# Opening of a two-layer hybrid decoder: lambda's vectors inside the packed parameters, first modulation tiles ahead of x, first norm by full products of ones

## The chip, the cores and the metric

One core of a Trainium2 chip runs the whole program. The metric is device time in microseconds (us) for one execution. Engines are named as in the profile: PE (TensorE matmul), PEld (its weight loads), DVE (VectorE), ACT (ScalarE), POOL (GpSimd), SP (SyncE, which here only issues DMAs).

## What is computed

Two layers of a trunk over a 256 x 1024 activation `x`, batch 1. Only the first steps of the first layer matter for the change; the rest is a sentence each.

```python
mod = silu(c) @ w_ada[l] + b_ada[l]                      # 1024 -> 6 x 1024: shift, scale, gate, twice
h = rmsnorm(x, norm1_g[l]) * (1 + sc1) + sh1
proj = h @ w_in[l]                                       # 1024 -> 2560: SSM input, two attentions' q, k, v
lam = exp(sum(lq1 * lk1)) - exp(sum(lq2 * lk2)) + lam_init   # a number per layer, vectors of 64
# S5 state space mixer, differential attention (uses lam), MoBA attention, w_out, gate, residual
# second norm with its own shift and scale, squared-ReLU MLP 1024 -> 4096 -> 1024, gate, residual
# after both layers: rmsnorm(x, final_g)
```

The decay factors of the state space mixer come from small parameter vectors (`a_re`, `a_im`, `log_dt`) by exponentials and sines.

## The kernel before

The activation is kept transposed: `xall` has 128 partitions, 8 feature tiles (`KT` = 8) and 256 time steps. A weight comes as a unit of 128 x 1024 fp32 (512 KB), loaded by SP into one of three `raw` buffers (L109). Each unit is split into a rounded high part (ACT, L123) and the remainder (DVE, L124), the activation likewise (`h_tile`, L432), and three products replace one fp32 product (`mm3`, L129).

All parameter vectors stand in one packed tile `par` (L72, columns given by `_COLS`). The lambda vectors do not: L1020 loads them with a DMA on ACT's queue that reads one row of 2 KB for each of the 128 partitions, and `ssm_params` multiplies and sums them on DVE (L498, L500), then feeds one exponential (`small_exp`, L502) that also yields the decay factors.

The opening runs over k = 0 to 7 (L1044). In round k, `ada_first(k)` (L318) loads two tiles of the modulation weights (buffers `ada`, three of them, `adaacc`, one, and `qT`, three, in turn), multiplies them on PE by the replicated silu(c) (`crep`) in four column strips, and ACT copies the result to `adarow`. `sums` brings it to columns of `mod`. `h_first(k-1)` builds the normed tile of the round before, and `proj_first(k-2)` adds its three groups of projections. On PE the order is: modulation of round k, projection of round k-2, sums of round k; so the first projection stands behind the modulation of the third round.

The first norm needs the mean square of x over features, which lie on partitions. `ssq_add` (L371) squares each of eight tiles on ACT and multiplies by ones, packed into four column strips of PE. `rms_bcast` (L380) copies the four partial sums, brings them to two columns by small matmuls with `sel` (L387), takes the root there (`rsqrt_cols`, ACT and four tiny DVE operations), and spreads the result by two transposes (L392) over all rows of a PSUM tile `pb`. Later norms use `x_norm` (L408): full products with a 128-column matrix of ones that put the sum in every row at once, one reciprocal root over 128 x 256 on ACT (L426) and a Newton step of three DVE operations over 128 x 256 (L427 to L429).

SP issues loads in the order of the program: `par`, four pieces of `x` (L78, 256 KB each), then for each round two modulation tiles (L330) and one weight unit (L109), each as its buffer comes free. A scheduler orders the other engines' instructions by when it believes that their inputs are ready, so small parameter work (`rope_tables`, `ssm_params`, L456 and L483, which stand behind the loop in the program) is spread between the opening's instructions on DVE. An engine's queue runs strictly in the order given.

Of the kernel before, what the change touches and what calls it, by code (L numbers as in the profile page):

```python
# [10 lines left out]
F32 = mybir.dt.float32  # L11
# [3 lines left out]
OP = mybir.AluOpType  # L15
# [26 lines left out]
for _name, _w in (("c", 8), ("a_re", 16), ("a_im", 16), ("ldt", 16), ("n1", 16), ("n2", 16), ("b_ada", 96),  # L42
                  ("d", 4), ("glu_b", 4), ("ssm_g", 4), ("subln", 2), ("moba", 2), ("fin", 8)):
    _COLS[_name] = (_n, _n + _w)
    _n += _w
# [8 lines left out]
@with_exitstack  # L54
def hybrid_trunk(ctx, tc, xT_d, pos_d, par_d, lqk_d, sb_d, sbt_d, scw_d, glu_d, wm_d, wa_d, out_d):
    nc = tc.nc
# [19 lines left out]
    xall = const.tile([128, KT, S], F32)  # L76
    for k in range(0, KT, 2):
        nc.sync.dma_start(xall[:, k:k + 2, :], xT_d[:, k:k + 2, :])  # L78
    xT = [xall[:, k, :] for k in range(KT)]
# [235 lines left out]

    last_row = [None]

    def ada_first(k):  # L318


        row = wk_tile()[:, :256]
        for h in range(2):
            i = (k * 2 + h) % 6
            if i < 3:
                w = ring.tile([128, UW], F32, name="ada", bufs=3)
            elif i < 4:
                w = big.tile([128, UW], F32, name="adaacc", bufs=1)
            else:
                w = work.tile([128, UW], F32, name="qT", bufs=3)
            nc.sync.dma_start(w, wa_d[k * 2 + h])  # L330
            for g in range(4):
                last_mm[0] = T.matmul(row[32 * g:32 * g + 32, :], crep[:, h * 4 + g, :], w[:, g * 256:(g + 1) * 256],
                                      start=(h == 0), stop=(h == 1), tile_position=(0, 32 * g), skip_group_check=True)
        rs = work.tile([128, 256], F32, name="adarow", bufs=1)
        last_row[0] = A.activation(rs, row, AF.Copy)
# [147 lines left out]
    def ssm_params():  # L483
# [11 lines left out]

        lq = lqt[:, :512].rearrange("p (l c d) -> p l c d", l=L, c=4)
        lp = work.tile([128, L, 2, 64], F32, name="qk", bufs=2)
        tt(lp, lq[:, :, 0:2, :], lq[:, :, 2:4, :], op=OP.mult)  # L498
        V.memset(ex[:, 16:32], 0.0)
        V.tensor_reduce(ex[:, 16:20], lp.rearrange("p l c d -> p (l c) d"), axis=mybir.AxisListType.X, op=OP.add)  # L500
        eo = const.tile([128, 32], F32)
# [516 lines left out]

    lqt = work.tile([128, 2 * 384], F32, name="at_e", bufs=4)
    nc.scalar.dma_start(lqt[:, :512], bass.AP(tensor=lqk_d.tensor, offset=lqk_d.offset, ap=[[0, 128], [1, L * 256]]))  # L1020
    ps = ssq_begin()
    for k in range(KT):
        ssq_add(ps, xT[k], k, KT)
    hs = []
# [19 lines left out]
    for k in range(KT):  # L1044
        if k == 0:
            sums = ada_first(k)
            pb = rms_bcast(ps, KT, 1.0 / D)
        else:
# [121 lines left out]
def _layout(inputs):  # L1170
# [17 lines left out]
    st["moba"] = cols(np.concatenate([g["moba_norm_g"], g["moba_norm_g"]], axis=1))  # L1188
    st["fin"] = cols(g["final_g"])
    par = np.empty((128, NCOL), f32)  # L1190
    for n, (a, b) in _COLS.items():
        par[:, a:b] = st[n]
    lqk = np.stack([g["diff_lq1"], g["diff_lq2"], g["diff_lk1"], g["diff_lk2"]], axis=1)
    lqk = np.ascontiguousarray(lqk.reshape(1, L * 256))
    sb = np.zeros((L, 128, 2, 2, 128), f32)
# [62 lines left out]
    wa[48:] = ada[1].transpose(2, 0, 1, 3).reshape(48, 128, UW)  # L1258
    return {"xT": xT, "pos": pos, "par": par, "lqk": lqk, "sb": sb, "sbt": sbt, "scw": sc, "glu": glu, "wm": wm, "wa": wa}

# [18 lines left out]
```

## Time and profile before

| | us |
|---|---|
| median of 3 timed runs | 690.89 |
| range of these runs | 690.33 to 696.8 |
| profiled execution, time | 694.18 |
| profiled execution, span | 692.5 |

The profile is of one execution. Its times count from the start of the span. A row of the timeline tells when a group of like instructions started, how long it lasted, on which engine, from which line, what it wrote from what, and how many there were; the bracket behind it tells how long the engine had been idle and what released it. Windows tell for a stretch how busy each engine was, the granted PE clock, the share of the 16 DMA engines and their rate. A matmul in fp32 leaves two records in this profile.

### The profile page before, as it was taken

Reading aid. Unit: us, or ns where it says so; the run is one execution under the profiler, and the core shown is the slowest. Engines: PE = TensorE matmul, PEld = TensorE weight load, DVE = VectorE, ACT = ScalarE, POOL = GpSimd, SP = SyncE. Lnnn points to the kernel's source line nnn. Section 1 sums busy time; section 2 is a strip of 40 time slices with the busy share of each in tenths; the row PEclk is TensorE's granted clock in tenths of the full one; section 3 lists DMA queues with packets and bytes.
Section 4 is the critical chain, followed back from the end, with each engine's and each line's share of the span. In section 5 each row is a group of like instructions: output and inputs, shape, how many; then the busy total and the mean of one; then the engine's idle time right before and its main releaser. Section 6 shows DMA issues by size and latency. Waiting matters only on the chain. (4 is left out here: it accounts for less than half of the span.)

```text
span 692.5 us, 13248 instructions
## 1 busy us (share of the span) xinstructions
PE 662.6 (96%) x5134; PEld 576.0 (83%) x5134; DVE 508.6 (73%) x1148; ACT 385.4 (56%) x730; POOL 19.2 (3%) x23
## 2 busy tenths in 40 slices
PE   4998999999999999999999999999999999999994
PEld 1785777988899888998887878799899988999883
DVE  5869879976997887868657799876875655555653
ACT  4557555664566833677443547576476633566540
POOL 0000000000000000000220000000000000000220
PEclk9999999999999999999999999999999999999998
DMA  8986786863889698879855632554356555555531
GB/s 299 405 314 210 256 301 219 297 224 117 310 300 320 217 336 257 292 282 327 308 183 182 213 123 64 166 183 147 113 163 203 183 183 183 183 183 183 188 117 61
DMA packets 45278, 152.22 MB, mean 220 GB/s; under 512 B 5152, under 2 KB 5280, under 8 KB 45216
## 3 DMA queue, kind: packets, MB, share of 16 engines
q1 hardware_dynamic: 44640, 150.60, 63.1%
q10 hardware_dynamic: 576, 0.79, 0.4%
q8 instruction: 40, 0.66, 0.4%
q14 instruction: 22, 0.18, 0.1%
HBM read 150.32 MB, written 1.05 MB: 219 GB/s over the span
## 5 line engine op out<-in xcount | busy, mean ns | idle before, releaser
L124 DVE TENSOR_TENSOR whl<-raw,whl 128x1024 fp32r<-128x1024 f32 x178 | 217.4, 1224 | 109.5 <-ACT whl L123 106.7
L123 ACT ACTIVATE whl<-raw 128x1024 fp32r<-128x1024 f32 x178 | 187.8, 1056 | 149.9 <-DMA raw<-in_wm_dram 51.0
L132 PE MATMUL wk<-hx,whl 128*128 128x256 f32 x1536 | 188.5, 284 | 2.2 <-DVE hx L440 1.2
L132 PEld LDWEIGHTS wk<-hx,whl 128*128 128x128 f32 x1536 | 185.4, 192 | 5.5 <-DVE hx L440 2.5
L991 PE MATMUL acc<-mx,whl 128*128 128x512 f32 x256 | 92.1, 399 | 0.0
L992 PE MATMUL acc<-mx,whl 128*128 128x256 f32 x256 | 71.9, 281 | 0.0
L991 PEld LDWEIGHTS acc<-mx,whl 128*128 128x128 f32 x256 | 48.1, 188 | 12.1 <-issue 0.8
L298 DVE SCALAR_TENSOR_TENSOR adaacc<-ada,cs,adaacc 128x1024 f32<-128x1024 f32 x35 | 44.8, 1280 | 9.2 <-DMA ada<-in_wa_dram 9.1
L132 PE MATMUL acc<-mx,whl 128*128 128x256 f32 x384 | 51.1, 288 | 0.0
L132 PEld LDWEIGHTS acc<-mx,whl 128*128 128x128 f32 x384 | 47.4, 191 | 2.8 <-issue 2.7
L992 PEld LDWEIGHTS acc<-mx,whl 128*128 128x128 f32 x256 | 48.4, 189 | 0.3 <-DVE whl L124 0.3
L991 PE MATMUL acc<-at_e,whl 128*128 128x512 f32 x128 | 46.6, 398 | 0.0
L994 DVE SCALAR_TENSOR_TENSOR xall<-acc,mod,xall 128x256 f32<-128x256 f32 x64 | 30.9, 482 | 21.0 <-PE acc L992 20.2
L132 PE MATMUL acc<-whl,hx 128*128 128x256 f32 x288 | 40.0, 288 | 0.0
L132 PEld LDWEIGHTS acc<-whl,hx 128*128 128x128 f32 x288 | 36.5, 191 | 3.1 <-issue 2.2
L784 PE MATMUL acc<-whl,hx 128*128 128x512 f32 x96 | 38.7, 403 | 0.0
L783 PE MATMUL acc<-whl,hx 128*128 128x512 f32 x96 | 38.2, 401 | 0.0
L785 PE MATMUL acc<-whl,hx 128*128 128x512 f32 x96 | 38.0, 396 | 0.0
L992 PE MATMUL acc<-at_e,whl 128*128 128x256 f32 x128 | 35.9, 280 | 0.0
L972 ACT ACTIVATE sp_pa<-wk 128x512 f32<-128x512 f32 x32 | 18.9, 590 | 28.0 <-PE wk L132 28.0
L991 PEld LDWEIGHTS acc<-at_e,whl 128*128 128x128 f32 x128 | 24.0, 188 | 5.9
L439 ACT ACTIVATE hx<-hz,mod 128x256 fp32r<-128x256 f32 x32 | 14.9, 502 | 21.1 <-DVE hz L434 21.1
(352 smaller groups left out, 986.9 us busy)
## 6 DMA issues: line engine op xcount, KB each, us to landing
raw<-in_wm_dram SPq DMA_DIRECT2D x184, 512.0 KB, 4.0
ada<-in_wa_dram SPq DMA_DIRECT2D x74, 512.0 KB, 5.6
sp_gc<-in_wa_dram SPq DMA_DIRECT2D x9, 256.0 KB, 5.1
qT<-in_wa_dram SPq DMA_DIRECT2D x4, 512.0 KB, 8.7
adaacc<-in_wa_dram SPq DMA_DIRECT2D x3, 512.0 KB, 7.8
qk<-in_wa_dram SPq DMA_DIRECT2D x6, 256.0 KB, 5.4
vv<-in_wa_dram SPq DMA_DIRECT2D x6, 256.0 KB, 3.8
at_o<-in_wa_dram SPq DMA_DIRECT2D x6, 256.0 KB, 4.5
```

The lines of the kernel that those rows point to most:

```text
L123: A.activation(hi, w, AF.Copy)
L124: V.tensor_tensor(lo, w, hi.bitcast(F32), op=OP.subtract)
L132: last_mm[0] = T.matmul(out, a[:, p, :], b[:, q, :], start=start and i == 0, stop=stop and i == 2, skip_group_check=True)
L298: V.scalar_tensor_tensor(acc, w, cs[:, k + j:k + j + 1], acc, op0=OP.mult, op1=OP.add)
L439: last_act[0] = A.activation(hi, z, AF.Identity, bias=mvec(l, i_sh, k))
L783: T.matmul(o, h[:, 0, sl], w[:, 0, :], start=(k == 0), stop=False, skip_group_check=True)
L784: T.matmul(o, h[:, 0, sl], w[:, 1, :], start=False, stop=False, skip_group_check=True)
L785: last_mm[0] = T.matmul(o, h[:, 1, sl], w[:, 0, :], start=False, stop=last, skip_group_check=True)
L972: A.activation(r, ps, AF.Relu)
L991: T.matmul(acc, w[:, 0, sl], a.rearrange("p c t -> p (c t)"), start=(k == 0), stop=False, skip_group_check=True)
L992: last_mm[0] = T.matmul(acc[:, :S], w[:, 1, sl], a[:, 0, :], start=False, stop=(k == 15), skip_group_check=True)
L994: V.scalar_tensor_tensor(xT[f], acc[:, c * S:(c + 1) * S], mvec(l, 5, f), xT[f], op0=OP.mult, op1=OP.add)
```

## The change

- The lambda vectors become four columns of `par` (`lq`, `lk`; layer by column, the first pair of vectors in partitions 0 to 63, the second in 64 to 127), and the DMA of L1020 goes. `ssm_params` multiplies them into a zeroed 128 x 4 tile, one PE product with ones sums over the partitions into PSUM, and DVE copies the four sums to the input of the exponential.
- The loading part of `ada_first` becomes a function of its own. Round 0's two modulation tiles are issued ahead of the four pieces of `x`.
- The first norm is a new `first_norm`: one product that adds epsilon, then eight full products of ones (four squares on ACT, four on DVE), and the root and Newton step as in `x_norm`. `pb` then lies in SBUF, not PSUM.
- `adarow` in `ada_first` takes the buffers of `sg_t` (two).

```diff
@@ _COLS
-                  ("d", 4), ("glu_b", 4), ("ssm_g", 4), ("subln", 2), ("moba", 2), ("fin", 8)):
+                  ("d", 4), ("glu_b", 4), ("ssm_g", 4), ("subln", 2), ("moba", 2), ("fin", 8),
+                   ("lq", 2), ("lk", 2)):
@@ hybrid_trunk, start
     xall = const.tile([128, KT, S], F32)
-    for k in range(0, KT, 2):
-        nc.sync.dma_start(xall[:, k:k + 2, :], xT_d[:, k:k + 2, :])
@@ ada_first
+    first_w = {}
+    def ada_first_load(k):
+        ws = []
         for h in range(2):
...
             nc.sync.dma_start(w, wa_d[k * 2 + h])
+            ws.append(w)
+        return ws
+    def ada_first(k):
+        row = wk_tile()[:, :256]
+        for h, w in enumerate(first_w.pop(k) if k in first_w else ada_first_load(k)):
             for g in range(4):
...
-        rs = work.tile([128, 256], F32, name="adarow", bufs=1)
+        rs = work.tile([128, 256], F32, name="sg_t", bufs=2)
@@ ssm_params
-        lq = lqt[:, :512].rearrange("p (l c d) -> p l c d", l=L, c=4)
-        lp = work.tile([128, L, 2, 64], F32, name="qk", bufs=2)
-        tt(lp, lq[:, :, 0:2, :], lq[:, :, 2:4, :], op=OP.mult)
+        lp = const.tile([128, 4], F32)
+        V.memset(lp, 0.0)
         V.memset(ex[:, 16:32], 0.0)
-        V.tensor_reduce(ex[:, 16:20], lp.rearrange("p l c d -> p (l c) d"), axis=mybir.AxisListType.X, op=OP.add)
+        for c in range(2):
+            r = slice(64 * c, 64 * c + 64)
+            tt(lp[r, c:4:2], col("lq", 0, 2)[r], col("lk", 0, 2)[r], op=OP.mult)
+        lps = wk_tile()[:, :4]
+        T.matmul(lps, ones[:, 0:1].to_broadcast([128, 128]), lp, start=True, stop=True)
+        V.tensor_copy(ex[:, 16:20], lps)
@@ opening
-    lqt = work.tile([128, 2 * 384], F32, name="at_e", bufs=4)
-    nc.scalar.dma_start(lqt[:, :512], bass.AP(tensor=lqk_d.tensor, offset=lqk_d.offset, ap=[[0, 128], [1, L * 256]]))
-    ps = ssq_begin()
-    for k in range(KT):
-        ssq_add(ps, xT[k], k, KT)
+    first_w[0] = ada_first_load(0)
+    for k in range(0, KT, 2):
+        nc.sync.dma_start(xall[:, k:k + 2, :], xT_d[:, k:k + 2, :])
+    def first_norm():
+        full = wk_tile()[:, :S]
+        T.matmul(full, sel.to_broadcast([128, 128]), epsd.to_broadcast([128, S]), start=True, stop=False)
+        for k in range(KT):
+            q = work.tile([128, S], F32, name="sq" if k % 2 == 0 else "so_y", bufs=3 if k % 2 == 0 else 2)
+            if k % 2 == 0:
+                A.activation(q, xT[k], AF.Square)
+            else:
+                V.tensor_tensor(q, xT[k], xT[k], op=OP.mult)
+            T.matmul(full, ones[:, 0:1].to_broadcast([128, 128]), q, start=False, stop=(k == KT - 1))
+        y = work.tile([128, S], F32, name="sq", bufs=3)
+        r = work.tile([128, 2, S], F32, name="sp_s", bufs=3)
+        t, pb = r[:, 0, :], r[:, 1, :]
+        A.activation(y, full, AF.Abs_reciprocal_sqrt, scale=1.0 / D)
+        V.scalar_tensor_tensor(t, full, -0.5 / D, y, op0=OP.mult, op1=OP.mult)
+        V.tensor_tensor(t, t, y, op=OP.mult)
+        V.scalar_tensor_tensor(pb, t, 1.5, y, op0=OP.add, op1=OP.mult)
+        return pb
@@ loop over k
             sums = ada_first(k)
-            pb = rms_bcast(ps, KT, 1.0 / D)
+            pb = first_norm()
```

## Rows read from the trace of the kernel before

**Rows 1.** The page, part 1: busy time, share of the span, instructions.

```profile
PE 662.6 (96%) x5134; PEld 576.0 (83%) x5134; DVE 508.6 (73%) x1148; ACT 385.4 (56%) x730; POOL 19.2 (3%) x23
```

**Rows 2.** Windows: stretch, length, busy per engine, PE clock, DMA share, GB/s.

```profile
3.00:7.00 4.00, 0.00 (x0) 0.00 (x0) 1.07 (x16) 0.21 (x1) 0.00 (x0) 1.00 0.72 167
...
8.00:24.00 16.00, 13.73 (x79) 6.59 (x80) 14.16 (x119) 11.23 (x24) 0.00 (x0) 1.00 1.03 409
...
34.00:38.00 4.00, 4.00 (x38) 3.15 (x37) 3.10 (x6) 2.74 (x7) 0.00 (x0) 1.00 0.76 265
```

**Rows 3.** DMA queues, 2 to 7 us: packets, MB, share of 16 engines.

```profile
q1 hardware_dynamic: 423, 0.65, 44.2%
q10 hardware_dynamic: 283, 0.26, 31.2%
```

**Rows 4.** Waits, 0 to 60 us: us in total, times, longest.

```profile
DVE qk L498 <- DMA at_e<-in_lqk_dram: 4.1, 1, 4.1
```

**Rows 5.** Timeline of all engines: start, length, engine, line, out<-in, count.

```profile
9.02 0.16 DVE L217 SCALAR_TENSOR_TENSOR cs<-cs,par 128x8 f32<-128x8 f32 x1
...
32.65 0.64 PE L332 MATMUL wk<-ada,crep 128*32 128x256 f32 x8
...
33.10 0.61 PE L332 MATMUL wk<-adaacc,crep 128*32 128x256 f32 x8
```

**Rows 6.** Timeline of PE alone, 8 to 30 us.

```profile
8.48 1.72 PE L377 MATMUL wk<-sq,ones 128*32 128x256 f32 x6 [8.48 <-ACT sq L375]
...
13.48 0.63 PE L377 MATMUL wk<-sq,ones 128*32 128x256 f32 x1
...
17.33 0.66 PE L392 MATMUL wk<-ident,rms_r 128*128 128x128 f32 x2 [0.41 <-DVE e2p L188]
...
21.95 1.93 PE L332 MATMUL wk<-qT,crep 128*32 128x256 f32 x16
23.81 1.65 PE L132 MATMUL acc<-hx,whl 128*128 128x256 f32 x6
...
25.68 0.63 PE L784 MATMUL acc<-whl,hx 128*128 128x512 f32 x1
...
26.69 0.39 PE L784 MATMUL acc<-whl,hx 128*128 128x512 f32 x1
...
28.29 1.07 PE L332 MATMUL wk<-ada,crep 128*32 128x256 f32 x16
```

**Rows 7.** Line 417, a square on DVE: count, then ns min/median/max.

```profile
L417 DVE TENSOR_TENSOR sq<-xall x2: 425/426/426, 370.1 to 683.5; 128x256 f32<-128x256 f32 x2
```

**Rows 8.** Timeline of SP, the issue of loads, 0 to 40 us.

```profile
3.41 1.75 SPq L330 DMA_DIRECT2D ada<-in_wa_dram  x2
...
9.51 0.90 SPq L330 DMA_DIRECT2D qT<-in_wa_dram  x2
...
20.91 0.38 SPq L330 DMA_DIRECT2D adaacc<-in_wa_dram  x1
```

**Rows 9.** Timeline around 493 us, a later norm with full products.

```profile
493.48 1.13 PE L422 MATMUL wk<-qT,ones 128*128 128x256 f32 x4
...
494.44 0.59 PE L422 MATMUL wk<-sq,sel 128*128 128x256 f32 x2
...
495.07 0.39 ACT L426 ACTIVATE sq<-wk 128x256 f32<-128x256 f32 x1 [1.09 <-PE wk L422]
```

**Rows 10.** Issue to landing: adaacc issued at 20.91; the qT pair at 9.51.

```profile
adaacc<-in_wa_dram SPq DMA_DIRECT2D x1, 512.0 KB, 9.0
...
DMA to landing us min/median/max: 9.4/9.8/10.2
```

**Rows 11.** Timeline: the exponentials' operand, its users, and the state weights' matmuls.

```profile
13.86 0.18 DVE L180 TENSOR_SCALAR e2r<-ex 128x32 f32<-128x32 f32 x1
...
29.19 0.42 DVE L616 TENSOR_TENSOR sp_gc<-sp_gc,abr 128x256 f32<-128x256 f32 x1
...
57.29 0.84 PEld L645 LDWEIGHTS wk<-ident,sp_gc 128*32 128x32 f32 x30 [0.27 <-DVE sp_gc L621]
```

More of the change, by code (lines that the diff above doesn't have):

```diff
@@ L54, in hybrid_trunk @@
 @with_exitstack
-def hybrid_trunk(ctx, tc, xT_d, pos_d, par_d, lqk_d, sb_d, sbt_d, scw_d, glu_d, wm_d, wa_d, out_d):
+def hybrid_trunk(ctx, tc, xT_d, pos_d, par_d, sb_d, sbt_d, scw_d, glu_d, wm_d, wa_d, out_d):
     nc = tc.nc
@@ L316, in hybrid_trunk @@
     last_row = [None]
-    def ada_first(k):
-        row = wk_tile()[:, :256]
+    first_w = {}
+    def ada_first_load(k):
+        ws = []
         for h in range(2):
@@ L1189, in _layout @@
     st["fin"] = cols(g["final_g"])
+    st["lq"] = cols(np.concatenate([g["diff_lq1"], g["diff_lq2"]], axis=1))
+    st["lk"] = cols(np.concatenate([g["diff_lk1"], g["diff_lk2"]], axis=1))
     par = np.empty((128, NCOL), f32)
@@ L1192, in _layout @@
         par[:, a:b] = st[n]
-    lqk = np.stack([g["diff_lq1"], g["diff_lq2"], g["diff_lk1"], g["diff_lk2"]], axis=1)
-    lqk = np.ascontiguousarray(lqk.reshape(1, L * 256))
     sb = np.zeros((L, 128, 2, 2, 128), f32)
@@ L1258, in _layout @@
     wa[48:] = ada[1].transpose(2, 0, 1, 3).reshape(48, 128, UW)
-    return {"xT": xT, "pos": pos, "par": par, "lqk": lqk, "sb": sb, "sbt": sbt, "scw": sc, "glu": glu, "wm": wm, "wa": wa}
+    return {"xT": xT, "pos": pos, "par": par, "sb": sb, "sbt": sbt, "scw": sc, "glu": glu, "wm": wm, "wa": wa}
 def kernel(**inputs):
```

## The prediction

> **What bounds the kernel now.** I read the page first: the tensor engine (PE) is busy for 96% of the span [rows 1], so after its start the kernel runs as long as PE has instructions, and an opening that is shorter by some microseconds moves all that follows by as much. The question is then only how far the opening can shrink, and what takes over as its limit. The reader should look at three things there.
>
> First, the DMA. Between 3 and 7 us the sixteen engines moved 167 GB/s although they were 72% occupied; from 8 to 24 us they moved 409 GB/s without a gap, and only between 34 and 38 us does the stream thin out [rows 2]. In the slow stretch a second queue, q10, moves 283 packets and 0.26 MB in 31.2% of the time, beside 423 packets of q1 in 44.2% [rows 3]. That is the lambda load of line 1020: one 2 KB row read by 128 partitions, issued from ACT. By these rows a byte on q10 takes almost twice the DMA time of one on q1.
>
> Second, the vector engine (DVE). It stands still for 4.1 us on exactly that load [rows 4], because line 498 sits in its queue ahead of the conditioning vector; so L217, a few operations on par, runs at 9.02 us [rows 5].
>
> Third, PE itself. Its timeline [rows 6] shows the norm's packed products from 8.48 to 14.1 us, the two transposes of L392 at 17.33, the modulation matmuls of the third round (16 records, qT) at 21.95, the first projection matmul at 23.81 and the fourth round at 28.29. From there one round takes 4.36 us, since the fifth starts at 32.65 [rows 5], and PE has no gap. Up to 26 us PE is slow as well: L784 takes 0.63 us at 25.68 and 0.39 at 26.69, and sixteen records of L332 take 1.93 us at 21.95 against 1.07 at 28.29 [rows 6]. The windows print a granted clock of 1.00 for the whole stretch [rows 2]; the durations say that the lower of the two levels (1.2 GHz) lasts until about 26 us, after a stretch of short products and pauses, and the upper (2.4 GHz) holds afterwards.
>
> **The change, part by part.**
>
> *Lambda from par.* This takes away the q10 load, L498 and L500 (a 128x256 operation is 0.42 us [rows 7]; two of them 0.84). It adds four columns to a load of 208 columns, a memset, two tiny products, one copy (four DVE operations of some 0.16 us, by L217's row) and one small fp32 matmul on PE, which is idle until the first data land. The load cost 0.26 MB. Bounds of what its absence gives back to the stream: if the slow stretch belongs to the first packets of any stream, only 0.26 MB at 409 GB/s, 0.64 us; if it belongs to q10, the other 0.41 MB of the 0.67 MB moved between 3 and 7 us need 1.0 us in place of 4, so 3.0 us. The stream's thin stretch at 34 to 38 us, with no q10 in it, still ran at 265 GB/s [rows 2], so part of such slowness comes with starting over. I take 2.0 us.
>
> *Order of loads.* Modulation tiles 0 and 1 (2 x 512 KB) go ahead of x (4 x 256 KB) on SP. Nothing is added, so every byte behind both is unmoved; x itself comes behind 1.05 MB instead of 0.26 MB. Before, x was issued ahead of the tiles, which followed from 3.41 us [rows 8]. With the rate taken above the first piece of x lands near 7.2 us: 3.0, plus 1.3 MB at 409 GB/s, 3.2, plus 1 for a slow start. Bounds 6.2 (no slow start) and 9 (slow as now). SP's instructions behind are the same and none waits for anything new. What the tiles gain: their matmuls run on PE before x is there and free two of the three "ada" buffers early, where now the norm's products stand in the same PE queue.
>
> *First norm.* Removed: eight packed products, a copy, four small matmuls (L387), five tiny DVE/ACT steps, two transposes. Added: nine full 128-column products; half the squares go from ACT to DVE (0.42 us there [rows 7], about as long on ACT), one 128x256 reciprocal root on ACT and three 128x256 DVE operations. The same code runs at 493 us: six records, which are three products, take from 493.48 to 495.03, so 0.52 us each, and the root 0.39 [rows 9]. Nine products cost 4.7 us at the upper level and, by the ratio of L332's rows (1.93 to 1.07), 8.5 at the lower. They run back to back from about 7.7 us, a square after the first landing. I take half of them at each level, 6.6 us, so the sum stands at 14.3; bounds 12.4 and 16.2. Then root 0.4, three DVE operations with their hand-overs 1.4, hz 0.5, hx 0.5 and 0.3 of semaphores: 3.1 us, so the first projection could start at 17.4. DVE's added work (four squares 1.7, Newton 1.3, less 0.84 and less four tiny steps) is about 2 us; the 4.1 us it no longer waits cover that, but some small parameter operations will still stand in front: I add 1.0, giving 18.4 us against 23.81. That is a gain of 5.4 us on the PE side. Without the cover DVE's 2 us would come off it.
>
> A row on the packed form speaks against this part: sixteen L332 records, eight products in column strips, take 1.07 us [rows 6], whereas two full products take 1.04. The Trainium skill (TensorE: Matmul & The Clock Gate, Part 3: Packing small matmuls) says that products with few output columns, put in different column strips, run at once; by it the full form costs PE about four times as much, which the trace agrees with, and it would make this norm longer by some 6 us at the lower level were PE the limit. The packed norm, however, was waiting for squares, and from its last record (13.48 + 0.63) to the end of the transposes (17.33 + 0.66) went 3.9 us of copies, small matmuls and roots [rows 6].
>
> *What is late next.* The stream. The second tile of the fifth round (adaacc, issued at 20.91) took 9.0 us to land [rows 8, 10], at 29.9; PE used it at 33.10 [rows 5], 3.2 us later. The third round's tiles, issued from 9.51, landed by 20.2 [rows 10] against 22.4 for its use in the second half of the 21.95 row. Later rounds have no less slack. In a saturated stream a landing moves only by what the stream was given, so the fifth round gains at most 3.2 + 2.0 = 5.2 us (bounds 3.8 and 6.2). The opening's gain is the smaller of 5.4 and 5.2; as either can come out lower I subtract 0.5 and take 4.7 us.
>
> **Sum.** The profiled execution took 694.18 us with a span of 692.5; less 4.7 it is 689.5. The median of the timed runs is 690.89, 3.3 us below the profiled one, so the same gain makes it 690.9 - 4.7 = 686.2 us. About 1% is what a measurement of this kernel can tell from no change, that is 6.9 us; my forecast stays inside it.
>
> **The rivals.**
>
> *The stream starts as slowly as before.* For it: x's own packets come first in a cold stream. Against it: the share of q10 and the recovery as it ends. The stream then gains 0.64 us, x lands near 9, the products end near 16, the first projection starts near 20.5. Gain about 3: 687.9 us.
>
> *The full products take back what the packed ones gave.* All nine at the lower level end at 16.2, and DVE, whose queue is in order, stalls: two buffers for its squares make the third wait for the first product, and the small parameter operations wait behind it. With 2 us of that the first projection starts at 21.3 to 22.5. Gain 1.3 to 2.5, say 689.0. This is where the skill's packing rule would lead; the trace bears it out in PE time, and less in the path.
>
> *Slower: lambda's matmul comes late.* The lambda part stands in the program behind all projections. Should its matmul be queued there on PE (near 47 us), the copy, the exponentials and everything from the decay factors on hang on it. In the trace the products of line 616 run at 29.19, long before their place in the code, and the state weights' matmuls of L645 already wait for DVE at 57.29 [rows 11]. The chain from the operand of the exponentials to those products now lies between 13.86 and 29.19 [rows 11]; some 12 us of it and 6 us of 128x256 products behind 47 us would reach 65, so 8 us of idle PE less the gain of about 4: 695 us. It decides once the matmul lands later than about 39 us. Against it: PE is idle when its operands are ready, at 4 us.
>
> *More than the stream allows.* If the later landings follow earlier buffer releases by more than I allow, or the clock's upper level from 12 us on speeds up every opening round: gain over 6.9, 683.5.
>
> **How the numbers follow.** Chances: forecast 0.50 (gain 3.3 to 6.2, 684.7 to 687.6), slow stream 0.15, products 0.17, no change for another reason 0.05, more than 6.9 us 0.08, lambda late 0.05. Range: from 684.2, just past the forecast's own best case, to 690.0, which takes in the slow stream and most of the products rival; it leaves out about 0.2. Faster by over 1% is the 0.08, slower by over 1% half of the lambda case and some mishap, 0.04, and 0.88 remains for within 1%.
>
> **What the profile after should show.** No q10 packets before the output; more than 300 GB/s between 3 and 7 us (else the slow-stream rival). L217 near 4 us and no long DVE wait before x. The modulation matmuls of the first round before the norm's products; nine products of two records each ending between 13 and 16 us, with short records toward their end (else the products rival). The lambda matmul before 8 us. The first projection near 18.4, the fourth round near 22.5, and from then on PE waiting for "ada" tiles for a microsecond in all, where now it never does. What makes the prediction wrong most easily is an order on DVE that puts the hz of the first round behind parameter work.

## The result

| | kernel before | changed kernel |
|---|---|---|
| median of timed runs, us | 690.89 (7 runs, 689.16 to 696.8) | 716.23 (7 runs, 709.8 to 718.82) |
| profiled execution, time and span, us | 694.18 and 692.5 | 709.8 and 708.1 |
| mean granted PE clock of the profiled execution | 0.997 | 0.981 |

The ratio is 1.036, with a 95% interval of 1.0327 to 1.0393: the change makes the kernel slower by 3.6%, where the forecast was 686.2 us and the range ended at 690.0. The profiled execution was the fastest of the seven; the median one ran with a mean granted clock of 0.972.

In the lines of the profile after, L338 are the modulation matmuls (L332 before), L1036 and L1043 the first norm's products, L509 is lambda's product, L626 the weight products (L616), L655 their transposes (L645), L686 the first state space matmuls (L676), L131 and L793 to L795 the projections (L132 and L783 to L785).

The page's part 1 answers [rows 1]: PE has the same work, in a longer span.

```profile
PE 666.0 (94%) x5132; PEld 580.6 (82%) x5132; DVE 514.1 (73%) x1153; ACT 384.3 (54%) x725; POOL 19.6 (3%) x23
```

Windows of the changed kernel (stretch, length, busy per engine, PE clock, DMA share, GB/s) answer [rows 2]:

```profile
3.00:7.00 4.00, 1.18 (x12) 0.55 (x16) 3.94 (x48) 1.96 (x5) 0.00 (x0) 1.00 0.97 313
8.00:24.00 16.00, 11.32 (x70) 8.61 (x71) 13.31 (x64) 8.43 (x17) 0.00 (x0) 0.97 1.03 410
23.00:26.00 3.00, 3.00 (x13) 2.71 (x12) 0.15 (x1) 0.00 (x0) 0.00 (x0) 0.50 1.05 416
57.00:61.00 4.00, 4.00 (x11) 3.09 (x11) 3.76 (x12) 1.11 (x2) 0.00 (x0) 0.57 0.63 211
82.00:189.00 107.00, 93.51 (x831) 73.55 (x834) 84.00 (x258) 56.19 (x151) 0.00 (x0) 0.94 0.62 208
94.00:101.00 7.00, 5.98 (x40) 3.34 (x40) 5.31 (x21) 2.25 (x9) 0.00 (x0) 0.55 0.74 255
130.00:137.00 7.00, 1.05 (x9) 0.85 (x8) 6.90 (x15) 1.54 (x2) 0.00 (x0) 0.90 0.85 277
137.00:142.00 5.00, 4.68 (x29) 4.08 (x29) 3.04 (x9) 1.42 (x3) 0.00 (x0) 0.50 0.79 286
```

The same stage in the kernel before, from the first state space matmul to the second norm:

```profile
60.00:171.00 111.00, 107.60 (x906) 86.23 (x906) 93.01 (x268) 64.67 (x159) 0.00 (x0) 1.00 0.69 242
```

The stream does what the forecast wanted (313 GB/s where it was 167). But between 82 and 189 us PE stands still for 13.5 us (107 less 93.51), against 3.4 before, and its clock is at the lower level (1.2 GHz) in stretches where before it stayed at the upper (2.4 GHz).

Where that comes from is in the timeline of the changed kernel (start, length, engine, line, out<-in, count; in brackets the idle time before and what ended it); it answers [rows 6, 11]:

```profile
4.15 0.16 DVE L507 TENSOR_TENSOR lp<-par 64x2 f32<-64x2 f32 x1
...
8.15 0.42 DVE L1042 TENSOR_TENSOR so_y<-xall 128x256 f32<-128x256 f32 x1 [0.54 <-DMA xall<-in_xT_dram]
9.84 1.22 PE L1036 MATMUL wk<-epsd,sel 128*128 128x256 f32 x2 [2.09 <-DVE sel L92]
15.11 1.22 DVE L123 TENSOR_TENSOR whl<-raw,whl 128x1024 fp32r<-128x1024 f32 x1
15.46 0.38 ACT L1047 ACTIVATE sq<-wk 128x256 f32<-128x256 f32 x1 [0.38 <-PE wk L1043]
17.60 0.42 DVE L1048 SCALAR_TENSOR_TENSOR sp_s<-wk,sq 128x256 f32<-128x256 f32 x1
20.12 0.38 PE L131 MATMUL acc<-hx,whl 128*128 128x256 f32 x1 [1.25 <-ACT hx L445]
21.59 0.86 PE L131 MATMUL acc<-hx,whl 128*128 128x256 f32 x5 [1.09 <-DVE hx L446]
...
53.73 0.28 PE L509 MATMUL wk<-lp,ones 128*128 128x4 f32 x2
54.05 0.16 DVE L510 COPY ex<-wk 128x4 f32<-128x4 f32 x1
54.33 0.17 DVE L179 TENSOR_SCALAR e2r<-ex 128x32 f32<-128x32 f32 x1
55.52 0.73 PE L793 MATMUL acc<-whl,hx 128*128 128x512 f32 x2 [1.51 <-DVE e2i L189]
57.95 0.63 PE L795 MATMUL acc<-whl,hx 128*128 128x512 f32 x1
...
62.99 0.18 DVE L192 TENSOR_SCALAR eo<-e2p 128x32 f32<-128x32 f32 x1
66.94 0.42 DVE L626 TENSOR_TENSOR sp_gc<-sp_gc,abr 128x256 f32<-128x256 f32 x1
...
76.20 0.39 PE L795 MATMUL acc<-whl,hx 128*128 128x512 f32 x1
77.17 0.27 PE L655 MATMUL wk<-ident,sp_gc 128*32 128x128 f32 x1 [0.58 <-DVE sp_gc L628]
82.05 1.16 PE L686 MATMUL wk<-uT,sb 32*128 32x128 f32 x16
...
137.32 1.11 PE L931 MATMUL wk<-ident,at_on 128*128 128x128 f32 x4 [6.27 <-DVE at_on L926]
```

Lambda's operands are ready at 4.3 us (a row of 0.16 us at 4.15). Its product runs at 53.73, behind the whole opening, and the exponentials that also give the decay factors stand behind it: the operand of the exponentials comes at 54.33 (before: 13.86), the first weight product at 66.94 (29.19), the first state space matmul at 82.05 (59.95). PE is hardly idle during this wait (2.6 us between 26 and 82 us), because the queue has projections of later groups to do (55.5 to 76.2 us, one row of many). That work, however, was what filled PE's waits in the next stage: of the 128x512 projection products, 94 records stood in that stage before and 10 do now, and PE has 831 instructions there where it had 906. For one attention step it now waits 8.3 us in all, 6.27 of them at once, where it waited 0.3, and it works at the lower level afterwards. The waits for that step, kernel before and changed kernel (us in total, times, longest):

```profile
PE wk L921 <- DVE at_on L916: 0.3, 1, 0.3
```

```profile
PE wk L931 <- DVE at_on L926: 8.3, 2, 6.3
```

By these rows the loss is paid there; no run tested this step by itself.

A ledger of the profiled executions, by the starts of four marks (fourth round of modulation; first state space matmul; root of the second norm; end), holds for all kernels that follow, with the median of the timed runs. All of them differ ahead of the second norm; what lies behind it takes 517 to 521 us in each.

| kernel | fourth round | state space | second norm | span | median |
|---|---|---|---|---|---|
| before | 28.29 | 59.9 | 171.3 | 692.5 | 690.89 |
| changed | 26.29 | 82.0 | 188.7 | 708.1 | 716.23 |
| 1 lambda early | 26.75 | 58.4 | 175.5 | 694.8 | 696.12 |
| 2 lambda part alone, late | 24.67 | 79.9 | 188.9 | 707.5 | 709.90 |
| 3 all but the lambda part | 29.78 | 61.4 | 180.8 | 699.6 | 698.52 |
| 4 PSUM buffer of its own | 28.34 | 60.0 | 180.4 | 700.6 | 701.06 |
| 5 lambda part alone, early | 26.09 | 57.7 | 167.9 | 686.1 | 688.02 |
| 6 early, old norm | 29.64 | 61.3 | 174.1 | 692.3 | 697.85 |
| 7 early, x first | 28.69 | 60.3 | 176.1 | 696.9 | 700.14 |
| 8 early, other epsilon | 29.78 | 61.4 | 173.3 | 692.7 | 691.41 |
| 9 as 8, squares on ACT | 26.99 | 58.6 | 173.2 | 691.7 | 695.13 |
| 10 as 1, squares on DVE | 28.36 | 60.0 | 170.3 | 691.3 | 693.05 |
| 11 exponentials apart | 27.76 | 59.4 | 174.4 | 694.0 | 695.43 |
| 12 lambda in the sixth round | 27.41 | 61.2 | 174.9 | 694.8 | 698.75 |
| 13 as 5, once more | 25.36 | 57.0 | 166.6 | 685.3 | 690.95 |
| 14 as 5, one product more | 25.35 | 58.9 | 175.7 | 696.1 | 690.79 |
| 15 the same, two rounds later | 25.31 | 60.1 | 172.9 | 691.4 | 694.34 |
| 16 as 15, three products | 25.70 | 63.1 | 174.2 | 692.6 | 697.45 |
| 17 as 5, three products more | 26.52 | 59.8 | 170.3 | 687.4 | 689.95 |
| 18 the same, another order | 24.96 | 58.3 | 169.8 | 687.0 | 691.75 |

Changed against before: 2.0 us won in the opening, 24.1 lost up to the state space matmul (55.7 against 31.6), 4.7 won in the next stage, whose projections were done already, 1.8 won behind: 15.6 us in sum, the difference of the two spans. The timed runs lose some 10 us more. Their median span is 714.5 us with a clock of 0.972; span times the missing share of the clock is 20 us. For the 114 runs of the kernel before that went beside the experiments the median span is 689.4 us with a mean clock of 0.991, so 6 us. By this estimate, which counts PE's pauses at the lower level as if it had worked in them, more than half of the 25 us is the lower level, the rest waiting.

### The profile page after: what moved, and what is told of

The parts are those of the page before. It is cut to its first block, busy times and chain, and to the rows that moved or that the text cites. A ratio compares the mean times of both kernels' runs of the same rounds, so it can differ in the third digit from the quotient of the medians.

```text
span 708.1 us, 13240 instructions
## 1 busy us (share of the span) xinstructions
PE 666.0 (94%) x5132; PEld 580.6 (82%) x5132; DVE 514.1 (73%) x1153; ACT 384.3 (54%) x725; POOL 19.6 (3%) x23
## 5 line engine op out<-in xcount | busy, mean ns | idle before, releaser
L131 PE MATMUL wk<-hx,whl 128*128 128x256 f32 x1536 | 188.3, 284 | 1.8 <-DVE hx L446 1.8
L131 PEld LDWEIGHTS wk<-hx,whl 128*128 128x128 f32 x1536 | 185.4, 192 | 5.0 <-DVE hx L446 3.1
L131 PE MATMUL acc<-mx,whl 128*128 128x256 f32 x384 | 51.9, 289 | 0.0
L131 PEld LDWEIGHTS acc<-mx,whl 128*128 128x128 f32 x384 | 47.7, 192 | 3.3 <-issue 2.7
L1004 DVE SCALAR_TENSOR_TENSOR xall<-acc,mod,xall 128x256 f32<-128x256 f32 x64 | 30.9, 482 | 21.6 <-PE acc L1002 20.8
L131 PEld LDWEIGHTS acc<-whl,hx 128*128 128x128 f32 x288 | 37.2, 194 | 4.0 <-issue 3.1
L131 PE MATMUL acc<-whl,hx 128*128 128x256 f32 x288 | 40.4, 290 | 0.0
L793 PE MATMUL acc<-whl,hx 128*128 128x512 f32 x96 | 38.7, 405 | 1.5 <-DVE e2i L189 1.5
L795 PE MATMUL acc<-whl,hx 128*128 128x512 f32 x96 | 38.6, 402 | 0.0
L872 ACT ACTIVATE at_e<-at_e,at_m 128x128 f32<-128x128 f32 (+1 forms) x48 | 21.2, 443 | 16.1 <-DVE at_m L867 16.1
```

Source lines behind the costliest of these rows:

```text
L131: last_mm[0] = T.matmul(out, a[:, p, :], b[:, q, :], start=start and i == 0, stop=stop and i == 2, skip_group_check=True)
L793: T.matmul(o, h[:, 0, sl], w[:, 0, :], start=(k == 0), stop=False, skip_group_check=True)
L795: last_mm[0] = T.matmul(o, h[:, 1, sl], w[:, 0, :], start=False, stop=last, skip_group_check=True)
L872: A.activation(e[:, c, ks], e[:, c, ks], AF.Exp, scale=SCALE, bias=mx[:, i:i + 1], accum_out=st[:, i:i + 1])
L1004: V.scalar_tensor_tensor(xT[f], acc[:, c * S:(c + 1) * S], mvec(l, 5, f), xT[f], op0=OP.mult, op1=OP.add)
```

## The experiments

The theory (A): lambda's product is late because of its place in PE's queue, and all loss comes from that. The first rival (B): new norm and order of loads lose as well. All ratios are to the kernel before on the same chip.

**1. Lambda early.** The changed kernel, with the sums written ahead of the first loads.

```diff
+    lambda_sums()          # memset, two tiny products, matmul, copy; taken out of ssm_params
     first_w[0] = ada_first_load(0)
```

> The changed kernel with one thing moved: the two lambda products, their sum over partitions on PE and the copy stand ahead of the first loads in the program, not inside the parameter function behind the loop. Theory A (the late sum over partitions, which the decay factors wait for, costs everything): the sum runs before 8 us, the first products of the decay factors near 30 us again, and the time falls below the kernel before by the 2 us by which the changed opening was already ahead at the fourth round: 686 to 690 us. Theory B (the new norm or the new order of loads costs it, for instance by a lower clock of PE): no change against the changed kernel, over 705 us.

**2. The lambda part alone**, on the kernel before, its sums in `ssm_params` as in the changed kernel.

```diff
-    nc.scalar.dma_start(lqt[:, :512], ...)        # and lqt, L498, L500
+        tt(lp[r, c:4:2], col("lq", 0, 2)[r], col("lk", 0, 2)[r], op=OP.mult)     # and the rest of it
```

> The kernel before with the lambda part of the change alone: vectors in the packed parameters, sum by a PE product inside the parameter function; norm and order of loads as before. Theory A: the product stands behind all projections (near 55 us) and the time is that of the changed kernel plus 2, 710 to 718 us. Theory B: within 3 us of the kernel before, 686 to 692.

**3. All but the lambda part**: the changed kernel with lambda's load and sums as before.

```diff
+    nc.scalar.dma_start(lqt[:, :512], ...)        # and lqt, tt, tensor_reduce as in the kernel before
     first_w[0] = ada_first_load(0)
```

> The changed kernel with the lambda part undone: the broadcast load on ACT's queue and the sums on DVE are back; tiles ahead of x and the full-product norm stay. Theory A: near the kernel before, 686 to 692 us, with DVE waiting for the load again. Theory B: over 705.

**4. A PSUM buffer of its own** for the product; its place in the program is unchanged.

```diff
-        lps = wk_tile()[:, :4]
+        lps = psum.tile([128, 512], F32, name="lps", bufs=1)[:, :4]     # wk: bufs=3
```

> The changed kernel with the lambda sum's PSUM tile taken from a buffer of its own, and the shared buffers of that kind cut from four to three; the product stays at its place in the program. If the sum comes late because the shared PSUM buffers go to their tiles in program order, it now runs before 8 us and the late state space stage is gone: 686 to 695 us (three shared buffers may cost some). If its place in the program alone makes it late, it stays near 53 us and the time over 705.

Measured: 696.12 us (1.0043, 1.0013 to 1.0073); 709.9 (1.0257, 1.0191 to 1.0323); 698.52 (1.0083, 1.0048 to 1.0118); 701.06 (1.0121, 1.0064 to 1.0179). The product of experiment 4, from PE's timeline:

```profile
4.34 0.59 PE L509 MATMUL lps<-lp,ones 128*128 128x4 f32 x2 [4.34 <-DVE lp L507]
```

Run 1 takes 20 of the 25 us away, run 2 brings 18 us to the kernel before (2.6%). With a buffer of its own the product runs at 4.34 instead of 53.73 us from the same place in the program: the tile takes its turn among the `wk` buffers that all groups share, and the place in the program decides the turn. So the late product is the main loss. But runs 1, 3 and 4 stand 0.4 to 1.2% (3 to 8 us) above before, between the two theories' ranges; by A alone they should not lose at all: A is not everything. Run 4 also has one shared buffer less, and what that costs was not measured by itself.

**11. Exponentials apart.** The product stays late, but the 16 columns of the decay factors no longer share an exponential with lambda's four.

```diff
-        small_exp(eo, ex, 32, "e2")
+        small_exp(eo[:, 0:16], ex[:, 0:16], 16, "e2")
+        small_exp(eo[:, 16:20], ex[:, 16:20], 4, "e3")
```

> The changed kernel, lambda's sums as late as in it, but the exponentials of the decay factors (16 columns) apart from those of lambda (4 columns). If the loss of the changed kernel runs from the late sums through the one shared exponential to the decay factors, the weight products come back to about 28 to 31 us, the first state space matmul to about 58 to 62, and the time to 694 to 700 us (PE has the second order here). If the late sums do their harm on another way (PE's queue itself, DVE's copy), the first state space matmul stays near 82 and the time at 710 to 718.

Measured: 695.43 us (1.0058, 1.0017 to 1.01). The lambda product by its line (count, ns, first and last start), and the first weight product in the timeline:

```profile
L509 PE MATMUL wk<-lp,ones x2: 167/210/253, 55.2 to 55.2; 128*128 128x4 f32 x2
```

```profile
28.66 0.42 DVE L627 TENSOR_TENSOR sp_gc<-sp_gc,abr 128x256 f32<-128x256 f32 x1
```

The product is as late as ever, 55.2 us, and the 20 us are gone. This shows the way of the loss: through the shared exponential to the decay factors, and not through PE's queue, DVE's copy or attention, which uses lambda much later.

**12. Lambda in the sixth round**, a place between the two.

```diff
+        if k == 5:
+            lambda_sums()
```

> The changed kernel with lambda's sums written in the sixth round of the opening, so that their product stands in PE's queue at about 31 to 35 us instead of 4 (early version) or 54 (changed kernel). By the 18 us that the prediction gave the chain from the sums to the state space matmuls, they would be ready by 53 and nothing waits: first state space matmul at 58 to 59, time as the early version, 695 to 697. By the 28 us that the changed kernel shows (53.7 to 82.0), the first state space matmul comes at 61 to 64, and the time is 697 to 702.

Measured: 698.75 us (1.0139, 1.0092 to 1.0186). From the timeline:

```profile
36.68 0.39 PE L499 MATMUL wk<-lp,ones 128*128 128x4 f32 x2
37.11 0.16 DVE L500 COPY ex<-wk 128x4 f32<-128x4 f32 x1 [0.50 <-PE wk L499]
45.02 0.42 DVE L629 TENSOR_TENSOR sp_gc<-sp_gc,abr 128x256 f32<-128x256 f32 x1
...
57.48 0.38 PE L658 MATMUL wk<-ident,sp_gc 128*32 128x128 f32 x2 [0.84 <-DVE sp_gc L631]
```

From the fourth round to the state space matmul it takes 33.8 us instead of the 31.6 of the kernel before and of runs 1 and 3 to 11: a product at 36.7 is late by 2.2 us already, and PE waits 0.84 us for the weight products. The prediction's 18 us ran from the product to the transposes of the weights, L645 (not to the state space matmul, as the expectation has it): here these are 20.8 us (36.68 to 57.48), in the changed kernel 23.4 (53.73 to 77.17). To the state space matmul it takes 24.5 and 28.3.

**5 to 8. What else costs.** The lambda part alone, early, on the kernel before; with the tiles ahead of x added; with the new norm added instead; and run 1 with epsilon by ones and a column of its own instead of `sel`. Runs 5 to 7 keep `adarow` in the two buffers of `sg_t` as well; run 2 does not. Shown against run 1:

```diff
     lambda_sums()
-    first_w[0] = ada_first_load(0)                       # runs 5 and 7
...
-            pb = first_norm()                            # runs 5 and 6
+            pb = rms_bcast(ps, KT, 1.0 / D)              # with ssq_begin and ssq_add as in the kernel before
# run 8
-        T.matmul(full, sel.to_broadcast([128, 128]), epsd.to_broadcast([128, S]), ...)
+        T.matmul(full, ones[:, 0:1].to_broadcast([128, 128]), eps128.to_broadcast([128, S]), ...)
```

> The kernel before with the lambda part alone (four columns of par, no load of lambda, adarow in sg_t's buffers), its sums written ahead of the loads of x so that the product is queued early; first norm and order of loads as before. Theory of the late sum alone: the part itself is harmless once early, and the q10 load is gone; 688 to 691 us. Theory that the remainder of 4 us in the version with early sums comes from the new norm or the order of loads: the same 688 to 691 here, with the lower clock level only where before had it. Theory that any new order of the instructions between 50 and 180 us meets a stall and a fall of the clock: 694 to 698.

> Lambda early and the modulation tiles ahead of x, but the first norm by packed products as before. If the new norm (its wait for sel, the hand-overs before hx) costs the remainder: 687 to 691 us. If the order of loads costs it: 694 to 698. If it is the order between 50 and 180 us that the scheduler makes anew each time: anywhere from 690 to 698, with falls of the clock behind stalls after 50 us.

> Lambda early and the new norm, but x loaded ahead of the modulation tiles as before. If the new norm costs the remainder: 694 to 698 us. If the order of loads does: 687 to 691. Products of the norm should start near 8.5 us, since x lands earlier, and run at the lower level longer, since no modulation products stand ahead of them.

> The changed kernel with early lambda sums, and the epsilon of the first norm by a column of its own in place of the product with sel, for which PE waited 1.5 us. If that wait and the late opening behind it are the remainder, the first projection comes 0.5 to 1 us earlier and the time is 693 to 695 us; if PE's stalls at 60 to 75 us (waits for modulation tiles) and the clock's fall behind them are it, nothing changes: 695 to 697.

Measured: 688.02 us (0.995, 0.9927 to 0.9973); 697.85 (1.0079, 1.005 to 1.0107); 700.14 (1.0093, 1.0058 to 1.0129); 691.41 (1.0003, 0.9979 to 1.0028). Run 13 timed version 5 once more:

> The version with the early lambda part alone once more, as the base of the next two on the same chip: 687 to 689 us, with no fall of PE's clock before the end.

It came out at 690.95 us (0.9977, 0.994 to 1.0014). The lambda part alone, done early, is thus the one part that gains anything, half a per cent in one comparison and nothing clear of noise in the other. Run 8 missed both of its expectations: its fourth round comes 3.0 us later than run 1's, and its median is 4.7 us lower. The first products of the squares in run 5, and those in run 6, from PE's timelines (every kernel has line numbers of its own; L383 is L377 of the kernel before):

```profile
5.31 4.20 PE L383 MATMUL wk<-sq,ones 128*32 128x256 f32 x14 [1.22 <-ACT sq L381]
```

```profile
9.05 1.37 PE L383 MATMUL wk<-sq,ones 128*32 128x256 f32 x5 [4.92 <-ACT sq L381]
```

Without the lambda load PE has the first squares at 5.31 us instead of the 8.48 of [rows 6]; two tiles ahead of x put them back to 9.05. In the ledger's first column: lambda part alone 26.09, plus order of loads 29.64, plus norm instead 28.69, both together 26.75. Seven profiles of kernels that are alike up to there (5, 13 to 18) lie between 24.96 and 26.52, so each of the two loses some 2 to 5 us by itself, and together they bring nothing over the lambda part. The buffers of `adarow` are not what gains: run 2, without them, has 24.67.

Run 3 shows what the lambda load did to the stream. It has the load back, with the tiles ahead of x:

```profile
3.00:7.00 4.00, 0.00 (x0) 0.00 (x0) 1.78 (x20) 1.49 (x2) 0.00 (x0) 1.00 0.93 312
```

That is the rate without the load (301 GB/s in run 5, 313 in the changed kernel), and lambda lands 5.1 us after its issue instead of 7.0. So the load by itself does not bring the 167 GB/s of [rows 2]; there it ran beside the pieces of x, and why that pair is slow no run shows. DVE still waits 2.2 us for the load in run 3.

The ledger's third column shows a second thing. From the state space matmul to the second norm it takes 110.2 to 111.9 us in before, 5, 8 and 10, and 112.8 to 120.4 in 1, 3, 4, 6, 7, 9, 11 and 12. PE has some 906 instructions there in all of them. Set side by side from the fourth round to the second norm (some 1,226 records), PE's instructions stand in one order in 5, 8 and 10, which before shares but for 20 records. Runs 1, 3, 6, 7 and 9 share a second order, 64 records apart from it (11 and 12 but for at most 20); run 4 has one of its own. In all with the second order SP issues two modulation tiles ahead of two weight units that were ahead of them before. Two groups of lines of PE in that stage, attention scores (L862) and state space (L689), with count, busy time and mean ns, run 5 and then run 6:

```profile
L862 PE MATMUL wk<-qT 64*128 64x128 f32 (+1 forms) x48 | 9.0, 356 | 0.0
...
L689 PE MATMUL wk<-uT,sb 32*128 32x128 f32 x64 | 6.5, 288 | 0.0
```

```profile
L862 PE MATMUL wk<-qT 64*128 64x128 f32 (+1 forms) x48 | 9.8, 356 | 0.0
...
L689 PE MATMUL wk<-uT,sb 32*128 32x128 f32 x64 | 7.7, 288 | 0.0
```

The same count at the same mean takes 2.0 us longer in sum, since fewer of these products on 32 or 64 rows overlap. The Trainium skill (TensorEngine Tiling (Array Packing), Tiling Modes: Key Properties) says that a change of tiling mode drains the engine while tiles of one mode work side by side; the trace agrees in direction, and no run here measured such a drain by itself. PE's busy time in the stage, from windows of run 5 and run 6:

```profile
58.00:168.00 110.00, 107.79 (x913) 86.19 (x914) 93.38 (x268) 64.60 (x160) 0.00 (x0) 1.00 0.70 244
```

```profile
61.00:174.00 113.00, 111.76 (x911) 87.77 (x909) 94.18 (x270) 66.18 (x161) 0.00 (x0) 1.00 0.69 238
```

Four microseconds more of PE for the same work, at a granted clock of 1.00. The theory of the order (C) from this: the other order costs the remainder.

**9 and 10. Tipping the order.** Version 8 with all squares on ACT takes the second order; version 1 with all squares on DVE takes that of before.

```diff
-            if k % 2 == 0:
+            if True:             # run 10: False
                 A.activation(q, xT[k], AF.Square)
```

> The version with early lambda sums and epsilon by its own column (691.4 us), with all eight squares of the first norm on ACT in place of four on each. This tips the scheduler: from PE's 294th instruction after the opening on (some 60 us), PE takes projections and modulation matmuls in the second order, that of the versions at 696 to 700 us, and SP issues two modulation tiles ahead of two weight units there, where the kernel before and the version at 691.4 have them the other way about. Theory of the order: 695 to 700 us, with PE's clock falling somewhere between 70 and 160 us. Theory that the opening alone makes the difference: 690 to 692, whatever the order behind it.

> The version with early lambda sums (696 us, PE's second order) with all eight squares of the first norm on DVE: DVE gets 1.7 us more to do in the opening, and the scheduler falls back to the order of the kernel before for all that follows. Theory of the order: 689 to 693 us although the opening is longer, with no fall of the clock between 40 and 600 us. Theory that the opening makes the difference: 696 to 699.

Measured: 695.13 us (1.005, 1.0013 to 1.0087) and 693.05 (1.0039, 1.0014 to 1.0064). Version 9 is 2.8 us ahead of version 8 in the fourth round and 0.2 us ahead at the second norm; version 10 is 1.6 us behind version 1 in the fourth round and 5.2 ahead at the second norm. In the ledger both go with the order. In the timed runs 9 leans that way (its interval and that of 8 just overlap), while the ratio of 10 cannot be told from that of version 1.

**14 to 16. One product more.** Version 5 with an extra product, which leaves the order alone in the fifth round and changes it in the seventh; run 16 has three.

```diff
+        if k == 4:      # runs 15 and 16: 6
+            zt = wk_tile()
+            for zz in range(1):      # run 16: 3, and stop=(zz == 2)
+                T.matmul(zt[:, :256], ones[:, 0:1].to_broadcast([128, 128]), xT[0], start=(zz == 0), stop=(zz == 0))
+            V.tensor_copy(ex[:, 28:32], zt[:, :4])
+            V.memset(ex[:, 28:32], 0.0)
```

> The version with the early lambda part alone, and one extra product of 128x256 (about 0.4 us of PE, result thrown away) in the opening's fifth round. PE's order behind the opening stays that of the kernel before. Both theories: 0.4 to 0.8 us above its base, 688 to 689.5.

> The same extra product, two rounds later. The scheduler then makes another order behind the opening (some 130 of PE's 4440 instructions and 10 of SP's 310 stand elsewhere); the opening up to there is the same. Theory of the order: the stage between the first state space matmul and the root of the second norm takes 112.5 to 118 us instead of 110.2, and the time is 691 to 697. Theory of the opening: 688 to 689.5, as with the product in the fifth round.

> Three such products in the seventh round (1.3 us of PE), for which the scheduler makes a third order (some 80 instructions of PE elsewhere). Theory of the order: 692 to 698 us. Theory of the opening: 689 to 690.

Measured: 690.79 us (0.9991, 0.9962 to 1.0019), 694.34 (1.003, 0.9995 to 1.0065), 697.45 (1.0102, 1.0065 to 1.0139). These don't decide: the extra product wrote into the tile of the exponentials' operand and so made the chain of run 12 late (first weight product at 39.5, 47.8 and 50.9 us, against 27.0 in run 5).

**17 and 18. The order alone.** Three extra products whose result goes to a column that nothing reads, in the seventh and in the eighth round.

```diff
+        if k == 6:      # run 18: 7
+            zt = wk_tile()
+            for zz in range(3):
+                T.matmul(zt[:, :256], ones[:, 0:1].to_broadcast([128, 128]), xT[0], start=(zz == 0), stop=(zz == 2))
+            dum = const.tile([128, 4], F32)
+            V.tensor_copy(dum, zt[:, :4])
```

> The version with the early lambda part alone and three extra products of 128x256 (some 1.3 us of PE) in the opening's seventh round, whose result goes to a column of its own that nothing else reads. The scheduler keeps the order of every other instruction as in its base. Both theories: 1 to 1.5 us above its base (688 to 691), so 689 to 692; the stage from the first state space matmul to the root of the second norm as in the base, 109.6 to 110.5 us.

> The same three products in the eighth round. Opening, lambda and exponentials stay as they are, and the work is the same; but the scheduler now makes another order behind the opening (some 128 of PE's 4442 instructions and 10 of SP's 310 elsewhere). Theory of the order: that stage takes 112.5 us or more, and the time is 693 to 699. Theory of the opening: as the run before, 689 to 692.

Measured: 689.95 us (1.0004, 0.9973 to 1.0034) and 691.75 (1.0001, 0.9983 to 1.002). The stage took 110.5 and 111.5 us, PE's busy time in windows of run 17 and run 18:

```profile
59.00:170.00 111.00, 108.45 (x911) 86.54 (x908) 93.94 (x271) 65.56 (x161) 0.00 (x0) 1.00 0.70 245
```

```profile
58.00:170.00 112.00, 109.99 (x915) 86.97 (x917) 93.78 (x272) 64.34 (x159) 0.00 (x0) 1.00 0.70 240
```

C falls as a general rule: another order is not slow by being another; this one costs 1 us in the profile and nothing that the timed runs can tell. For the second order the timed runs speak, if not each by itself: the kernels that have it stand at 1.0043 to 1.0093 (run 12, with its late product, at 1.0139), those with the order of run 5 at 0.995 to 1.0039. None of them, however, was had without a change in the opening.

The granted clock of the stage, by windows of every profile, divides the loss further. Where it is 1.00, the stage takes 109.5 to 111.9 us in the order of before (before, 5, 8, 10, 13, 17) and 111.2 to 113.7 in others (6, 12, 15, 16, 18). All longer ones have 0.96 to 0.99: 114.5 us in run 9, 115.8 in 7, 117.1 in 1 and 119.4 in 3, with PE's order the same as in run 6, and 116.7 in run 14, with that of run 5. So the second order costs some 1 to 4 us at full clock (runs 6 and 12 against the order of before), and what goes beyond comes with falls of the clock, which the order of before meets too in run 14. In runs 1 and 3 PE also waits 3.3 and 2.4 us there for modulation tiles, in run 6 0.5 (in before 2.6). The loss of version 1 lies in that stage (117.1 us against 111.4), not in its opening, which is 1.5 us ahead of before. Whether its order, the time at which the stage begins or chance brings the falls and the waits stays open.

## Why the prediction was wrong

**The step that failed** is the last sentence of the rival with the late lambda product: "PE is idle when its operands are ready, at 4 us". They were ready at 4.3 us, and that did not matter: in a queue with a fixed order what counts is the place, and the place came from the turn of the shared `wk` buffers (run 4), not from readiness. The evidence taken for an early place, line 616 at 29.19 [rows 11], was a DVE instruction that takes no such buffer. The case was named, with its chain and its place "near 47 us", and given 0.05.

**Its price** was short as well: 695 us for the case against 716. Its 18 us from the sums to the transposes of L645 were 23.4 in the changed kernel and 20.8 in run 12; so the point from which it decides was not 39 us but some 36.5 (57.3 less 20.8), and run 12 at 36.7 already lost 2.2. And it counted "8 us of idle PE", where PE was not idle: it used up the projections, and stood still later, with the clock falling behind the waits. Two matmuls of the same shape show what that costs: 0.63 us in the row at 57.95, 0.39 at 76.20. The Trainium skill (TensorE: Matmul & The Clock Gate, HAM oscillation — how this bites in real kernels) says that waits between groups of matmuls send the engine back to its slow clock, so that each group starts slow again; this trace agrees, with the 6.27 us wait and the 0.50 behind it.

**The opening.** The stream went as taken, or better: 0.00 MB on q10 and 313 GB/s; the slow-stream rival is out. The landing of x was taken at 7.2 and its first squares ran at 8.15; the norm's first product, taken at 7.7, waited for `sel` until 9.84, a small DVE operation that the prediction did not list, so the products ended at 15.4 instead of 14.3. (DVE's added work, "about 2 us", is 1.5 by the terms listed, 1.7 + 1.3 - 0.84 - 0.64; nothing was built on the difference.) The warned-of order on DVE came true: a weight split of 1.22 us and small parameter operations stood ahead of the Newton step, which began at 17.60, 1.8 us after its root. The first projection started at 20.12, not 18.4, and still waited 1.09 us for the second half of hx; then PE's clock fell (0.50 from 23 to 26 us), and the fourth round came at 26.29 instead of 22.5. Of the 4.7 us of gain 2.0 were left.

**Nothing is added** by the order of loads, the prediction said. The bytes were the same, but x came later, and with the old norm that cost 3.5 us of opening by itself (run 6 against run 5). "The full products take back what the packed ones gave" is what run 7 shows: with x first the new norm is 2.6 us slower than the packed one. The lambda load was the one thing whose removal gained time: by itself it brings the fourth round from 28.29 to 24.67 (run 2; 26.09 and 25.36 in runs 5 and 13), no less than the whole change, and back in the changed kernel it costs 3.5 us (29.78 against 26.29, run 3). The prediction's upper bound, 3.0 us, put the slow stretch on q10; run 3, with 312 GB/s beside the same load, does not bear that out.

**What the gain is worth.** Version 5 moves every mark up to the second norm by 2.2 to 3.5 us and the median by 3.2 and 0.6 us in two comparisons, of which only the first is clear of noise. So part of an earlier opening can reach the end, as the reading of [rows 1] said; how much is not settled.

## What to carry to other kernels

When a small product moves to an engine with an ordered queue, ask which buffer it takes and whose turn that is, before asking when its operands are ready; then follow everything that shares an instruction with its result. A wait that other work fills is not free: that work was the filler of a later wait, and the bill comes there, with the lower clock on top. A scheduler that places instructions anew after each edit makes a change in the opening a change of the stage behind it, so compare the order and the granted clock behind the edit before comparing times.

## What was not expected of the hardware

PE's clock fell without an idle PE as well. Windows of run 9, in which short products on 64 and 32 rows fill the first stretch:

```profile
99.00:103.00 4.00, 4.00 (x26) 3.19 (x26) 3.80 (x16) 2.16 (x11) 0.00 (x0) 1.00 0.81 226
103.00:108.00 5.00, 5.00 (x18) 3.93 (x18) 4.41 (x16) 2.54 (x9) 0.00 (x0) 0.66 0.09 39
```

And such a fall comes in some executions of a kernel and not in others. The profiled execution of run 14 took 697.85 us, the longest of its eleven, with 0.50 from 115 to 125 us and a mean clock of 0.982, where others of the eleven had up to 0.996; its stage from the state space matmul to the second norm took 116.7 us although its order is that of before:

```profile
115.00:125.00 10.00, 10.00 (x50) 7.63 (x43) 6.83 (x13) 3.58 (x6) 0.00 (x0) 0.50 0.74 266
```

Version 5 spread from 685.63 to 694.26 us in one comparison. The printed clock of the opening is to be read with care: runs 13 and 5 show 0.50 and 1.00 for the same stretch with the same kernel and much the same busy times; what tells the level there is the length of the matmuls (eight records of L338 take 1.08 us in both, at 16.11 and 16.00 us; 0.64 at 30 us).

```profile
13.00:22.00 9.00, 7.14 (x53) 4.01 (x46) 8.12 (x67) 5.39 (x11) 0.00 (x0) 0.50 1.03 407
```

```profile
13.00:22.00 9.00, 7.88 (x54) 4.37 (x55) 8.12 (x67) 5.82 (x13) 0.00 (x0) 1.00 1.03 407
```
